# A three-block ConvFFN: operands prepared in steps through DRAM, fewer weight pieces kept, weights loaded one unit ahead

## The chip, the core and the metric

The kernel runs on one core of a Trainium2 chip. Time is device microseconds (us) of one execution, from 3 runs, given as their median and spread. One further execution was profiled; every row below is of that one. Engines are named as the profile does: PE is TensorE's matmuls, PEld its weight loads, DVE is VectorE, ACT ScalarE, POOL GpSimd, SP SyncE, which here issues the DMAs (transfers).

## The reference

One decoder layer over 2048 prompt tokens and 32 sample tokens, model width 1024, FFN width 3072. What the change touches is the last sub-layer and the final norm:

```python
x = x + oc @ p['w_mem_o']                       # cross-attention's projection
n3 = rmsnorm(x, p['g_ffn'])
g, ffn_state = causal_dwconv(n3 @ p['w_ffn_gate'], ffn_prev, p['w_ffn_conv'], p['b_ffn_conv'])
x = x + (jax.nn.gelu(g) * (n3 @ p['w_ffn_up'])) @ p['w_ffn_down']
...
y_prompt = rmsnorm(xp, g_final)
```

All of it is float32.

## The kernel before

**Products.** A float32 operand is held as two parts, hi (rounded for TensorE) and lo (the rest). `split` (L77, L81) makes them: hi by ACT, lo by DVE or POOL, which reads the source and hi. `mm3` (L135) multiplies hi·hi, hi·lo and lo·hi, three matmuls a product.

**Phases.** Phase 0 makes the memory's keys and values, phase 1 is the mixer, phase 2 the output projection and cross-attention over four token blocks s = 0 to 3 of 512 (the samples ride along with others). `memo` (the projection `pmo`) ends a phase-2 block: it adds to the residual x, stores it to DRAM (`x2d`, L1183), and POOL sums its squares (`ssum`, L1196); `rstd3` (L1199) turns them into 1/rms and stores that (`r3d`, L1201).

**The FFN** (`phase3`) runs three token blocks, `SB3`: 696, 692 and 660 + 32 tokens. Each has 24 gate units f and 12 down units d; a down takes two gate units' results. The order of a block is f0, f1, f2, d0, f3, f4, d1, and so on to d9 after f20; then f21, f22, f23; blocks 0 and 1 then make the next block's operands (`"n"` in the plan), run d10 and d11, and normalise and store the block (`final`); block 2 ends in `tail`.

A gate unit (`_P3.gate_up`) computes gate and up projection together by a scheme of seven products instead of eight: both halves of the input's width and both halves of the tokens are combined. Its operands are the seven combinations of `BUDDY` (b11, t2, t1, t3, b21, b22, t4) for four k each; its weights are the pieces a11, s2, s1, s3, a12, s4, a22, of which the s are sums and differences of the weights. Each product is 12 matmuls of 346 to 348 columns into PSUM (`pg`); ACT copies two of them out (`u`, `gb`, L1311 and L1321), DVE adds the others (L1294), then come the convolution (`gc`: ACT L1335, DVE L1337), the gelu, the product `up` and its split `ah`, `al`. A down (`_P3.down`) is 96 matmuls into `pd` from four weight pieces; DVE adds the result to the residual `acc` (L1361).

**Operands.** `p3_norm(s)` loads x by `p3_load`, multiplies by gain and 1/rms (L708), forms the combinations (L693) and splits them (every third lo by POOL) into 56 tiles in SBUF that stay for the whole block. For block 0 it is called ahead of everything in `phase3`, with a priority of 400 (`N3_PRIO`).

**Weights.** `piece_stream` yields pieces of 128 x 2 x 512 (hi, lo), and `piece(ahead=4)` holds up to five at hand, over six buffers `wpc`. In block 0 it loads raw weights, splits them, and stores every piece to DRAM (`kept_g`, seven a gate unit; `kept_d`, four a down; L574); in blocks 1 and 2 it loads each piece from there (`again`), 512 KB a piece.

**What sets the order.** The Tile framework schedules the program's operations onto each engine's queue by priority and dependence; each engine, and SP's DMA queue, then runs its queue in order.

Of the kernel before, what the change touches and what calls it, by code (L numbers as in the profile page):

```python
# [45 lines left out]
class _Kernel:  # L46
# [3 lines left out]
    def run(self):  # L50
        nc, tc, I = self.nc, self.tc, self.I
        with ExitStack() as es:
# [12 lines left out]
            with ExitStack() as e2:  # L65
                self.wspl = e2.enter_context(tc.tile_pool(name="wspl", bufs=3))
                self.psa = e2.enter_context(tc.tile_pool(name="psa", bufs=1, space=bass.MemoryType.PSUM))
                self.psb = e2.enter_context(tc.tile_pool(name="psb", bufs=1, space=bass.MemoryType.PSUM))
                self.phase0()
                self.phase1()  # L70
                self.phase2()
# [393 lines left out]
    def phase2(self):  # L465
        with ExitStack() as es:
# [31 lines left out]
            smp = _MemSample(self)  # L498
            for s in range(4):
# [13 lines left out]
                step(SMO)  # L513
                p.qproj(1)
                step(SMO)
                p.score(0)
# [3 lines left out]
                step(SMO)  # L520
                p.score(1)
                p.trans(0)
                p.qproj(3)
                step(SMO)
                p.score(2)
# [3 lines left out]
                step()  # L529
                p.score(3)  # L530
# [3 lines left out]
                step()  # L534
                p.trans(3)
                p.pv(2)
                nx(2)
                step()
                p.pv(3)
                nx(3)  # L540
                step()
                for u in range(4):
                    p.memo(u)
                    step()
                step()
# [3 lines left out]
                p.rstd3()  # L549

    def piece_stream(self):

# [4 lines left out]
        def load(src):  # L557
            raw = self.wraw.tile([128, 1024], F, name="wr", tag="wr")
            nc.sync.dma_start(raw, src)
            return raw[:, 0:512], raw[:, 512:1024]  # L560
# [6 lines left out]
        def new():  # L567
            return self.wpc.tile([128, 2, 512], R, name="pc", tag="pc")
# [8 lines left out]
        def again(key):  # L577
            t = new()
# [3 lines left out]
        def paired(f):  # L582
            a11, a12 = load(I["w_gate"][f])
            a21, a22 = load(I["w_up"][f])
            yield halves(("g", f, 0), a11, "pool")
            s1 = sums(a21, a22, OP.add)
            s2 = sums(s1, a11, OP.subtract)
            yield halves(("g", f, 1), s2, "dve")
            yield halves(("g", f, 2), s1, "pool")
            yield halves(("g", f, 3), sums(a11, a21, OP.subtract), "dve")  # L590
            yield halves(("g", f, 4), a12, "pool")
            yield halves(("g", f, 5), sums(a12, s2, OP.subtract), "dve")
            yield halves(("g", f, 6), a22, "pool")

        def plain(c):
            raws = [load(I["w_down"][c * CH + i]) for i in range(CH)]
            for h in range(2):
                for i in range(CH):
                    yield halves(("d", c, h * CH + i), raws[i][h], "pool")

        for kind, i in self.units:
            n = 7 if kind == "g" else 2 * CH
            if (kind, i, 0) in kept:
                for e in range(n):
                    yield again((kind, i, e))
            else:
                yield from paired(i) if kind == "g" else plain(i)
# [10 lines left out]
    def phase3(self):  # L618
        nc, tc, I, O = self.nc, self.tc, self.I, self.O
        NC = NF // CH  # L620
        with ExitStack() as es:
# [12 lines left out]
            self.n3 = [None] * 3  # L634
            with tc.high_priority(N3_PRIO):
                self.n3[0] = self.p3_norm(0)
# [4 lines left out]
            for s in range(3):  # L641
# [5 lines left out]
                if s < 2:  # L647
                    plan += [("n", s + 1, 0), ("d", s, NC - 2), ("d", s, NC - 1), ("f", s, 0)]
# [3 lines left out]
            for kind, s, i in plan:  # L652
                if kind == "g":
                    if i == 0:
                        sb = _P3(self, s)
                    acts[i] = sb.gate_up(i)
                    if i == 1:
                        sb.load_acc()
                elif kind == "d":
                    sb.down([acts[i * CH + e] for e in range(CH)])  # L660
                elif kind == "n":
                    self.n3[s] = self.p3_norm(s)
                else:
                    sb.final()
            sb.tail([acts[NF - CH + e] for e in range(CH)])

    def p3_load(self, s, k):
        t0, w, smp = SB3[s]
        W = w + (NS if smp else 0)
        if s and k % 4 > 1:  # L670
            x = self.wraw.tile([128, W], F, name="x3", tag="wr")
        else:
            x = self.xs.tile([128, W], F, name="x3", tag="x", bufs=4)
        self.p3_dma(x, [d[k] for d in self.x2d], t0, W)
        return x
# [9 lines left out]
    def p3_norm(self, s):  # L685
        nc, q1 = self.nc, self.xs
# [3 lines left out]
        rt = q1.tile([128, W], F, name="rt3")  # L690
        self.p3_dma(rt, self.r3d, t0, W)
        self.n3n, ops = 0, {}
# [11 lines left out]
        def norm(k):  # L704
            xs = []
            for kk in (k, k + KT // 2):
                x = self.p3_load(s, kk)
                nc.vector.scalar_tensor_tensor(x, x, self.col(G_FFN, kk), rt, op0=OP.mult, op1=OP.mult)  # L708
                xs += [x[:, 0:H], x[:, H:W]]
            return xs  # L710

        def steps(k, b11, b12, b21, b22):
            put("b11", k, b11)
            t1 = q1.tile([128, H], F, name="t3", tag="t", bufs=4)
            sub(t1, b12, b11)
            sub(b12, b22, b12)
            sub(b11, b12, b11, OP.add)
            yield
# [12 lines left out]

        if s == 0:
            for k in range(KT // 2):
# [809 lines left out]
```

## Time and profile before

| | |
|---|---|
| runs, median (lowest to highest) | 2776.86 us (2772.53 to 2779.53) |
| the profiled execution: time, span | 2779.39 us, 2777.5 us |
| mean granted TensorE clock | 0.969 |
| busy share of the span: PE, DVE, ACT, POOL | 94%, 56%, 34%, 20% |
| moved by DMA | 619.88 MB, mean 223 GB/s |
| chain that ended last, by engine | PE 72%, DVE 13%, DMA 4%, ACT 4%, issue 3% |

The span is the profiled execution from its first to its last instruction; 1.9 us lie around it. Busy shares are averages over all stages. The chain is the work that ended last, followed back from the end, step by step, to whatever released each piece; "issue" is time in which an engine waited for nothing that the profile shows.

### The profile page before, as it was taken

What the parts mean: (1) busy time and instruction counts of PE and PEld (TensorE: products, weight loads), DVE (VectorE), ACT (ScalarE), POOL (GpSimd) and SP (SyncE); (2) the same over time, 40 slices, a digit from 0 to 9 for tenths busy, and PEclk for the clock granted to TensorE, in tenths of its full rate; (3) what the DMA queues carried; (4) which work ended last, traced back from release to release, by engine and by line L of the source; (5) the groups of instructions that cost most, each with busy time, mean ns of one, the idle gap of its engine ahead of it and who ended that gap; (6) DMA issues with size and microseconds to landing.
All of it is one profiled execution on the core that took longest, in us unless ns stands there. A gap on an engine that the chain in (4) does not pass through costs nothing.

```text
span 2777.5 us, 40472 instructions
## 1 busy us (share of the span) xinstructions
PE 2620.8 (94%) x15221; PEld 2414.7 (87%) x15221; DVE 1556.6 (56%) x2735; ACT 945.0 (34%) x1831; POOL 543.7 (20%) x586
## 2 busy tenths in 40 slices
PE   6999998998999996999999978999999989999997
PEld 5777877977998884899999978999999889999997
DVE  6567776676442536767666674544444644444445
ACT  5464735475332434343434342111111321111112
POOL 3422312022402013333333351000000300000001
PEclk9899999999999997999999989999999999999999
DMA  6764544367757565787777758666676576676664
GB/s 244 258 220 147 174 159 151 135 232 252 272 173 247 183 210 181 262 298 273 300 270 292 278 211 284 226 219 220 211 232 209 170 269 223 209 233 211 215 223 147
DMA packets 211650, 619.88 MB, mean 223 GB/s; under 512 B 30404, under 2 KB 51140, under 8 KB 211456
## 3 DMA queue, kind: packets, MB, share of 16 engines
q1 hardware_dynamic: 211456, 617.30, 64.1%
q8 instruction: 121, 1.98, 0.3%
q14 instruction: 73, 0.60, 0.1%
HBM read 442.31 MB, written 174.90 MB: 222 GB/s over the span
## 4 chain that ended last, share of the span: by engine, by line
PE 72%; DVE 13%; DMA 4%; ACT 4%; issue 3%; POOL 2%; SPq 1%; POOLq 0%; ACTq 0%; DVEq 0%
PE pg L135 27%; PE pd L135 17%; PE pin L135 9%; PE po L135 6%; PE pmo L135 3%; PE pq L135 3%; DVE gc L1337 2%; PE sc L135 1%; ACT gc L1335 1%; DVE n L81 1%; POOL pc L81 1%; PE tp L804 1%; DVE pc L81 1%; DVE gb L1294 1%; PE pa L135 1%
## 5 line engine op out<-in xcount | busy, mean ns | idle before, releaser
L135 PE MATMUL pg<-n,pc 128*128 128x346 f32 (+1 forms) x6048 | 1036.7, 330 | 55.4 <-DVE up L1294 18.5
L135 PEld LDWEIGHTS pg<-n,pc 128*128 128x128 f32 x6048 | 979.6, 192 | 101.4 <-DVE up L1294 31.1
L135 PE MATMUL pd<-ah,pc 128*128 128x346 f32 (+1 forms) x2240 | 468.9, 325 | 21.4 <-DVE acc L1361 21.3
L135 PEld LDWEIGHTS pd<-ah,pc 128*128 128x128 f32 x2240 | 378.5, 191 | 29.1 <-DVE acc L1361 27.0
L1361 DVE TENSOR_TENSOR acc<-pd,acc 128x692 f32<-128x692 f32 (+1 forms) x280 | 245.4, 877 | 150.4 <-PE pd L135 149.9
L135 PE MATMUL pd<-al,pc 128*128 128x346 f32 (+1 forms) x1120 | 272.4, 324 | 0.0
L135 PE MATMUL pin<-n1h,wh 128*128 128x512 f32 (+1 forms) x560 | 188.5, 363 | 14.6 <-DVE ql L81 8.7
L135 PEld LDWEIGHTS pd<-al,pc 128*128 128x128 f32 x1120 | 197.0, 191 | 0.0
L81 POOL TENSOR_TENSOR pc<-wr,pc 128x512 fp32r<-128x512 f32 x120 | 161.2, 1346 | 156.5 <-ACT pc L77 147.9
L1337 DVE SCALAR_TENSOR_TENSOR gc<-gb,pp,gc 128x696 f32<-128x696 f32 (+2 forms) x144 | 147.1, 1021 | 79.6 <-ACT gc L1335 77.1
L135 PE MATMUL pin<-n1l,wh 128*128 128x512 f32 (+1 forms) x560 | 186.6, 359 | 4.7 <-DVE n1l L81 4.7
L135 PE MATMUL pin<-n1h,wl 128*128 128x512 f32 (+1 forms) x560 | 185.8, 358 | 2.6 <-POOL wl L81 1.7
L1331 POOL COPY fcarry<-gb 128x2 f32<-128x2 f32 x72 | 14.2, 198 | 875.0 <-DVE gb L1294 873.7
L1294 DVE TENSOR_TENSOR up<-pg,u 128x346 f32<-128x346 f32 (+1 forms) x144 | 74.2, 515 | 148.6 <-PE pg L135 148.6
L1294 DVE TENSOR_TENSOR u<-pg,u 128x346 f32<-128x346 f32 (+1 forms) x144 | 74.5, 518 | 141.6 <-PE pg L135 140.4
L1321 ACT ACTIVATE gb<-pg 128x346 f32<-128x346 f32 (+1 forms) x72 | 33.2, 461 | 338.4 <-PE pg L135 338.4
L135 PEld LDWEIGHTS pin<-n1h,wh 128*128 128x128 f32 x560 | 103.6, 194 | 32.5 <-DVE ql L81 9.3
L1311 ACT ACTIVATE u<-pg 128x346 f32<-128x346 f32 (+1 forms) x72 | 32.5, 452 | 285.4 <-PE pg L135 285.2
L1294 DVE TENSOR_TENSOR gb<-pg,u 128x314 f32<-128x314 f32 (+2 forms) x96 | 38.9, 426 | 160.1 <-PE pg L135 160.1
L81 POOL TENSOR_TENSOR wl<-wr,wh 128x1024 fp32r<-128x1024 f32 x35 | 85.9, 2461 | 208.5 <-ACT wh L77 193.1
L135 PEld LDWEIGHTS pin<-n1l,wh 128*128 128x128 f32 x560 | 103.1, 194 | 19.9 <-DVE n1l L81 5.8
L135 PEld LDWEIGHTS pin<-n1h,wl 128*128 128x128 f32 x560 | 103.1, 194 | 18.7 <-POOL wl L81 2.1
(319 smaller groups left out, 4203.4 us busy)
## 6 DMA issues: line engine op xcount, KB each, us to landing
pc<-kept_g SPq DMA_DIRECT2D x336, 512.0 KB, 4.3
kept_g<-pc SPq DMA_DIRECT2D x168, 512.0 KB, 3.1
pc<-kept_d SPq DMA_DIRECT2D x96, 512.0 KB, 4.4
wh<-keeph SPq DMA_DIRECT2D x90, 512.0 KB, 3.7
wl<-keepl SPq DMA_DIRECT2D x90, 512.0 KB, 4.7
kept_d<-pc SPq DMA_DIRECT2D x48, 512.0 KB, 3.6
x<-in_x_dram SPq DMA_DIRECT2D x72, 256.0 KB, 5.0
keeph<-wh SPq DMA_DIRECT2D x30, 512.0 KB, 3.5
```

Of the source, the lines that this page charges most:

```text
L81: e.tensor_tensor(out=lo, in0=src, in1=hi.bitcast(F), op=OP.subtract)
L135: nc.tensor.matmul(o, w[a], xs, start=first and n == 0, stop=last and n == 2, skip_group_check=more)
L804: nc.tensor.transpose(tp[:, j], st[:, j, c * 128:(c + 1) * 128], K.ident)
L1294: add = lambda o, p, t: nc.vector.tensor_tensor(out=o, in0=p, in1=t, op=OP.add)
L1311: nc.scalar.activation(u, X, AF.Copy)
L1321: nc.scalar.activation(gb[:, 2:2 + H], X, AF.Copy)
L1331: nc.gpsimd.tensor_copy(self.carry[:, f], gb[:, w:w + 2])
L1335: nc.scalar.activation(gc, gb[:, 2:2 + NW], AF.Identity, scale=K.col(C_FW, 48 + f), bias=K.col(C_FB, f))
L1337: nc.vector.scalar_tensor_tensor(gc, gb[:, k:k + NW], K.col(C_FW, 24 * k + f), gc, op0=OP.mult, op1=OP.add)
L1361: nc.vector.tensor_tensor(out=v, in0=pd[:, :, 0:H], in1=v, op=OP.add)
```

## The change

- **Operands ahead, in steps.** `p3_norm` becomes `p3_prep(s)`, a generator of 32 steps that writes the split combinations to DRAM (`opd{s}_{i}`, one per combination) through two-buffer tiles `n3s`. Block 0's steps run inside phase 2, in its blocks s = 2 and 3; those of block s+1 inside the gate units 4 to 19 of FFN block s, after products 1 and 4 of each.
- **Loaded by product.** `p3_ops(s, i)` loads one whole operand (128 x 8 x H, 1.42 MB) in one DMA: for block 0 at the FFN's start, for the others after the product of f23 that last reads the old one.
- **Weights.** Only the four sums of a gate unit are kept in DRAM (`kept_s`). a11, a12, a22 and all down pieces are loaded raw and split at every use, hi by ACT and lo by POOL; later blocks load only the second half of w_up. `raws` loads a unit's raw weights during the unit before.
- **Norms in steps.** The last down of blocks 0 and 1 takes the sums of squares (`sums`); `final` and the 1/rms of phase-2 block 3 (`rstd3_steps`) run as steps after the products of the next gate units 0 and 1.
- **Space.** Phase 2's `yraw` moves to the `wraw` buffers, `ssum3` of its last block to a new pool `prep`, which also holds 1/rms and one combination.

The core of the diff:

```diff
 def phase2(self):
+            self.xpool = lambda: dict(pool=self.wraw, tag="wr")
+            ready = self.p3_prep(0)
+
+            def prep(n=1):
+                if s > 1:
+                    for _ in range(n):
+                        next(ready, None)
                 p.qproj(0)
                 step(SMO)
+                prep()
...
-                p.rstd3()
+                if s < 3:
+                    p.rstd3()

 def piece_stream(self):
-        def halves(key, src, lo_eng):
-            t = new()
+        def halves(src, lo_eng):
+            t = self.wpc.tile([128, 2, 512], R, name="pc", tag="pc")
             self.split(src, t[:, 0], t[:, 1], "act", lo_eng)
+            return t
+
+        def keep(key, src, lo_eng="dve"):
+            t = halves(src, lo_eng)
             kept[key] = self.dram.tile([128, 2, 512], F, name="kept_" + "_".join(map(str, key)))
             nc.sync.dma_start(kept[key], t.bitcast(F))
             return t
...
+            if ("s", f, 0) in kept:
+                yield halves(a11, "pool")
+                for e in range(3):
+                    yield again(("s", f, e))
+                yield halves(a12, "pool")
+                yield again(("s", f, 3))
+                yield halves(u, "pool")
+                return
...
+        nxt = raws(*self.units[0])
+        for n, (kind, i) in enumerate(self.units):
+            now, nxt = nxt, None
+            for t in paired(i, *now) if kind == "g" else plain(now):
+                yield t
+                if nxt is None and n + 1 < len(self.units):
+                    nxt = raws(*self.units[n + 1])

 def phase3(self):
             with tc.high_priority(N3_PRIO):
-                self.n3[0] = self.p3_norm(0)
+                for i in range(7):
+                    self.p3_ops(0, i)
...
-                    plan += [("n", s + 1, 0), ("d", s, NC - 2), ("d", s, NC - 1), ("f", s, 0)]
+                    plan += [("d", s, NC - 2), ("d", s, NC - 1)]
...
                     if i == 0:
+                        rest = sb.final() if s else self.p2[3].rstd3_steps()
+                        ready = self.p3_prep(s + 1) if s < 2 else iter(())
                         sb = _P3(self, s)
-                    acts[i] = sb.gate_up(i)
+
+                    def after(e, s=s, i=i):
+                        if i < 2:
+                            next(rest, None)
+                        elif 4 <= i < 20 and e % 3 == 1:
+                            next(ready, None)
+                        if s < 2 and i == NF - 1:
+                            self.p3_ops(s + 1, e)
+
+                    acts[i] = sb.gate_up(i, after)

+    def p3_ops(self, s, i):
+        H = self.opd[s][0].shape[2]
+        t = (self.n3a if i < 2 else self.n3b).tile([128, KT, H], R, name=f"n3_{i}")
+        self.nc.sync.dma_start(t.bitcast(F), self.opd[s][i])
+        self.n3[i] = t

-    def p3_norm(self, s):
+    def p3_prep(self, s):
         def put(nm, k, src):
-            hl = []
-            for e in "hl":
-                n = BUDDY.index(nm) * 8 + k * 2 + "hl".index(e)
-                hl.append((self.n3a if n < 26 else self.n3b).tile([128, H], R, name=f"n3_{n}"))
-            self.split(src, hl[0], hl[1], "act", "pool" if self.n3n % 3 == 0 else "dve")
-            self.n3n += 1
-            ops[nm, k] = hl
+            nonlocal n
+            t = tile_([128, 2, H], R, "n3s")
+            self.split(src, t[:, 0], t[:, 1], "act", "pool" if n % 3 == 0 else "dve")
+            n += 1
+            nc.sync.dma_start(self.opd[s][BUDDY.index(nm)][:, 2 * k:2 * k + 2], t.bitcast(F))

 class _P3
         def down(self, acts, sums=False):
...
+            if sums:
+                self.tot = K.sumsq(K.xs, acc[:, m], self.tot if m else None, self.W, tags=(("x", 4),) * 2)

     def final(self):
-        tot = None
-        for m in range(KT):
-            tot = K.sumsq(K.xs, acc[:, m], tot, self.W, tags=(("x", 4),) * 2)
-        rt = K.rstd(K.xs, tot, self.W, "pd", "rt3")
+        rc = K.rstd_cols(K.xs, self.tot, self.W, "pd")
+        yield
+        rt = K.rstd_rows(K.xs, rc, self.W, "pd", "rt3")
+        yield
         for m in range(KT):
             nc.vector.scalar_tensor_tensor(acc[:, m], acc[:, m], K.col(G_FIN, m), rt, op0=OP.mult, op1=OP.mult)
             nc.sync.dma_start(K.O["y"][m, :, self.t0:self.t0 + self.W], acc[:, m])
+            yield
```

How the engines' queues change, at three places. First SP at the end of phase 2 and the start of the FFN: `x2d` are stores of the residual, `rt` and `x` loads for the operands. Before:

```order
L1183 DMA x2d_70<-x_6_9845 128x512
L681 DMA rt_10503<-r3d_71 128x512
L681 DMA rt_10503<-r3d_72 128x184
L681 DMA x_10506<-x2d_67 128x512
L681 DMA x_10506<-x2d_68 128x184
L681 DMA x_10510<-x2d_67 128x512
L681 DMA x_10510<-x2d_68 128x184
```

Of the change, `n` being the operand tiles:

```order
L1224 DMA x2d_70<-x_7_9993 128x512
L680 DMA fst<-in_ffn_conv_dram 128x384
L607 DMA kept_s_0_10705<-pc 128x1024
L728 DMA n_2_10668<-opd_2_8859 128x2784
L728 DMA n_3_10670<-opd_3_8860 128x2784
L728 DMA n_4_10672<-opd_4_8861 128x2784
L728 DMA n_5_10674<-opd_5_8862 128x2784
L728 DMA n_6_10676<-opd_6_8863 128x2784
```

The loads of x and 1/rms for the first operands have left this place; operands 2 to 6 are loaded behind the last store of the residual, and operands 0 and 1 stand some twenty rows earlier.

Second DVE at the end of FFN block 0, from gate unit 23 into the last two downs. Before:

```order
L1294 TENSOR_TENSOR up<-pg,u_15735 128x348
L1337 SCALAR_TENSOR_TENSOR gc<-gb,pp,gc 128x696
L1361 TENSOR_TENSOR acc<-pd,acc 128x696
L708 SCALAR_TENSOR_TENSOR x_15862<-x_15862,pp,rt_15843 128x692
L1339 TENSOR_TENSOR up<-up,gc 128x696
L708 SCALAR_TENSOR_TENSOR x_15866<-x_15866,pp,rt_15843 128x692
L708 SCALAR_TENSOR_TENSOR x_15870<-x_15870,pp,rt_15843 128x692
L81 TENSOR_TENSOR al<-up,ah 128x696
L708 SCALAR_TENSOR_TENSOR x_15874<-x_15874,pp,rt_15843 128x692
L81 TENSOR_TENSOR n_5_15895<-x_15862,n_4_15894 128x346
L693 TENSOR_TENSOR t_15898<-x_15862 128x346
```

Of the change:

```order
L1387 SCALAR_TENSOR_TENSOR gc<-gb,pp,gc 128x696 x2
L1342 TENSOR_TENSOR up<-pg,u_15719 128x348
L1411 TENSOR_TENSOR acc<-pd,acc 128x696
L1389 TENSOR_TENSOR up<-up,gc 128x696
L1411 TENSOR_TENSOR acc<-pd,acc 128x696
L83 TENSOR_TENSOR al<-up,ah 128x696
L1411 TENSOR_TENSOR acc<-pd,acc 128x696 x14
```

The norm (L708), the combinations (L693) and the lo halves (L81 on `n`) that stood among and behind the gate unit's last steps are gone from here, and the downs' accumulates follow each other.

Third ACT in FFN block 1, around a gate unit's end, where the steps for block 2 run. Before:

```order
L1338 ACTIVATE gc<-gc 128x692
L77 ACTIVATE ah<-up 128x692
L1311 ACTIVATE u<-pg 128x346
L1321 ACTIVATE gb<-pg 128x346
L1335 ACTIVATE gc<-gb,pp 128x692
```

Of the change:

```order
L1388 ACTIVATE gc<-gc 128x692
L79 ACTIVATE ah<-up 128x692
L79 ACTIVATE n3s<-x_16859 128x346
L79 ACTIVATE pc<-wr 128x512
L79 ACTIVATE n3s<-x_16859 128x346
L79 ACTIVATE n3s<-t_16927 128x346
L1361 ACTIVATE u<-pg 128x346
L79 ACTIVATE pc<-ws 128x512
L79 ACTIVATE pc<-wr 128x512
L79 ACTIVATE n3s<-x_16859 128x346
L79 ACTIVATE n3s<-x_16864 128x346
L1371 ACTIVATE gb<-pg 128x346
```

Hi halves of weight pieces (`pc`) and of operands (`n3s`) now stand among the copies out of PSUM.

## Rows read from the trace of the kernel before

**Rows 1.** The page's list of engines, busy time with its share of the span and the number of instructions.

```profile
PE 2620.8 (94%) x15221; PEld 2414.7 (87%) x15221; DVE 1556.6 (56%) x2735; ACT 945.0 (34%) x1831; POOL 543.7 (20%) x586
```

**Rows 2.** The trace in windows cut at the stages (end of phase 2; FFN start; block 0; its end; start of block 1; block 1; start of block 2). Columns: window, its length, busy time with number of instructions of PE, PEld (TensorE's weight loads), DVE, ACT, POOL, then the granted TensorE clock, the busy share of the DMA engines and GB/s.

```profile
1010.00:1073.00 63.00, 61.82 (x311) 50.48 (x310) 29.53 (x68) 24.69 (x60) 8.56 (x7) 1.00 0.36 131
1073.00:1176.00 103.00, 73.45 (x366) 65.21 (x365) 79.68 (x105) 42.97 (x77) 39.44 (x38) 0.78 0.72 260
1176.00:1580.00 404.00, 394.01 (x2380) 376.64 (x2380) 270.88 (x370) 157.59 (x254) 149.66 (x145) 1.00 0.77 285
1580.00:1676.00 96.00, 78.14 (x443) 75.16 (x442) 65.41 (x90) 41.47 (x74) 49.72 (x39) 0.89 0.60 221
1676.00:1748.00 72.00, 64.72 (x374) 61.37 (x373) 36.85 (x52) 14.26 (x21) 4.64 (x9) 0.95 0.82 286
1748.00:2139.00 391.00, 389.02 (x2377) 380.07 (x2376) 177.78 (x246) 61.12 (x90) 6.63 (x36) 1.00 0.66 218
...
2221.00:2294.00 73.00, 62.90 (x371) 59.92 (x370) 33.60 (x53) 14.08 (x20) 5.24 (x14) 0.95 0.77 258
```

**Rows 3.** The chain of waits over the whole span, its longest pieces: start, duration, what. `pmo` is the last memory projection of phase 2, `pd` a down unit, `pg` a gate unit's product.

```profile
1055.64 17.81 PE pmo L135 x77
...
1171.98 4.31 PE pd L135 x24
...
1575.83 4.09 PE pd L135 x24
...
1648.75 27.64 PE pd L135 x156
...
1733.10 15.25 PE pd L135 x96
...
1777.30 14.56 PE pd L135 x91
...
2124.93 14.56 PE pd L135 x91
...
2191.50 29.59 PE pd L135 x168
...
2280.24 14.30 PE pd L135 x90
...
2714.03 14.30 PE pd L135 x90
```

**Rows 4.** The same chain between the last memory projection and the first operands.

```profile
1075.41 1.71 POOL ssum L1196
...
1087.13 2.02 DMA r3d<-rt
```

**Rows 5.** Groups of instructions by form from 1073 to 1116 us, where the first operands are made: line, engine, operation, out<-in, shapes and count, then busy us, mean ns of one, and the idle time before them with what ended it.

```profile
L77 ACT ACTIVATE n<-x 128x348 fp32r<-128x348 f32 x24 | 10.9, 486 | 21.3 <-DMA r3d<-rt 9.1 <-DVE x L693 9.1 <-DVE x L708 3.0
...
L81 POOL TENSOR_TENSOR n<-x,n 128x348 fp32r<-128x348 f32 x9 | 9.9, 1108 | 20.2 <-ACT n L77 18.6 <-DMA acc<-x2d 1.5
L81 DVE TENSOR_TENSOR n<-x,n 128x348 fp32r<-128x348 f32 x15 | 9.8, 680 | 0.1
L708 DVE SCALAR_TENSOR_TENSOR x<-x,pp,rt 128x696 f32<-128x696 f32 x8 | 8.5, 1059 | 0.0
L693 DVE TENSOR_TENSOR x<-x,x 128x348 f32<-128x348 f32 x8 | 4.8, 603 | 0.1
```

**Rows 6.** Three stretches of 10 us, one at the FFN start and two at the start of block 1; columns as in rows 2.

```profile
1690.00:1700.00 10.00, 8.02 (x37) 7.49 (x38) 5.08 (x7) 0.84 (x2) 0.00 (x0) 0.83 1.00 366
...
1720.00:1730.00 10.00, 7.58 (x45) 6.91 (x44) 1.84 (x4) 0.46 (x1) 0.00 (x0) 1.00 1.04 392
...
1090.00:1100.00 10.00, 4.92 (x12) 3.18 (x12) 9.60 (x14) 5.13 (x13) 5.42 (x5) 0.50 0.66 228
```

**Rows 7.** The chain at the end of block 0.

```profile
1644.04 3.00 DVE n L81 x7
...
1647.90 0.80 DVE acc L1361
```

**Rows 8.** A wait in the steady part of block 0 (1313 to 1580 us): who waited, and for whom, us in total, times, longest.

```profile
PEld pd L135 <- DVE acc L1361: 5.2, 10, 1.2
```

**Rows 9.** Groups by form in the same stretch of block 0, six periods; columns as in rows 5.

```profile
L81 POOL TENSOR_TENSOR pc<-wr,pc 128x512 fp32r<-128x512 f32 x61 | 80.8, 1325 | 92.4 <-ACT pc L77 91.7
...
L1361 DVE TENSOR_TENSOR acc<-pd,acc 128x696 f32<-128x696 f32 x49 | 42.8, 874 | 5.6 <-PE pd L135 5.6
L77 ACT ACTIVATE pc<-wr 128x512 fp32r<-128x512 f32 x60 | 37.7, 629 | 69.5 <-issue 28.5 <-PE pg L135 21.8 <-PE pd L135 11.9
...
L1337 DVE SCALAR_TENSOR_TENSOR gc<-gb,pp,gc 128x696 f32<-128x696 f32 x24 | 27.4, 1143 | 13.6 <-ACT gc L1335 13.2
...
L81 DVE TENSOR_TENSOR al<-up,ah 128x696 fp32r<-128x696 f32 x12 | 12.0, 1001 | 5.2 <-ACT ah L77 5.1
```

**Rows 10.** The same groups of DVE in block 1 (1792 to 2053 us), six periods.

```profile
L1361 DVE TENSOR_TENSOR acc<-pd,acc 128x692 f32<-128x692 f32 x49 | 43.0, 878 | 34.7 <-PE pd L135 34.5
...
L1337 DVE SCALAR_TENSOR_TENSOR gc<-gb,pp,gc 128x692 f32<-128x692 f32 x24 | 22.6, 940 | 14.7 <-ACT gc L1335 14.2
...
L81 DVE TENSOR_TENSOR al<-up,ah 128x692 fp32r<-128x692 f32 x12 | 10.5, 875 | 5.1 <-ACT ah L77 5.1
```

**Rows 11.** The page's list of DMA issues: out<-in, queue, kind and count, KB each, median us from issue to landing.

```profile
kept_g<-pc SPq DMA_DIRECT2D x168, 512.0 KB, 3.1
```

More of the change, by code (lines that the diff above doesn't have):

```diff
@@ L559, in load, with raws @@
             nc.sync.dma_start(raw, src)
-            return raw[:, 0:512], raw[:, 512:1024]
+            return raw
+        def raws(kind, i):
+            if kind == "d":
+                return [load(I["w_down"][i * CH + e]) for e in range(CH)]
+            g = load(I["w_gate"][i])
+            if ("s", i, 0) not in kept:
+                return g, load(I["w_up"][i])
+            u = self.wsum.tile([128, 512], F, name="ws", tag="ws")
+            nc.sync.dma_start(u, I["w_up"][i][:, 512:1024])
+            return g, u
         def sums(x, y, op):
@@ L577, in again, with paired @@
         def again(key):
-            t = new()
+            t = self.wpc.tile([128, 2, 512], R, name="pc", tag="pc")
             nc.sync.dma_start(t.bitcast(F), kept[key])
             return t
[L582 to L585, printed above, removed]
+        def paired(f, g, u):
+            a11, a12 = g[:, 0:512], g[:, 512:1024]
+            if ("s", f, 0) in kept:
[6 more added lines that the diff above has]
+                return
+            a21, a22 = u[:, 0:512], u[:, 512:1024]
+            yield halves(a11, "pool")
@@ L601, in piece_stream @@
[L601 to L607, printed above, removed]
+            yield keep(("s", f, 0), s2)
+            yield keep(("s", f, 1), s1, "pool")
+            yield keep(("s", f, 2), sums(a11, a21, OP.subtract))
+            yield halves(a12, "pool")
+            yield keep(("s", f, 3), sums(a12, s2, OP.subtract))
@@ new lines, in paired, with plain @@
+            yield halves(a22, "pool")
+        def plain(rs):
+            for h in range(2):
+                for r in rs:
+                    yield halves(r[:, h * 512:h * 512 + 512], "pool")
+        nxt = raws(*self.units[0])
[5 more added lines that the diff above has]
+                    nxt = raws(*self.units[n + 1])
@@ L730, in steps @@
             put("t4", k, b21)
-        if s == 0:
-            for k in range(KT // 2):
-                for _ in steps(k, *norm(k)):
-                    pass
-        else:
-            runs = [steps(k, *x) for k, x in enumerate([norm(k) for k in range(KT // 2)])]
-            for _ in BUDDY:
-                for r in runs:
-                    next(r, None)
-        return ops
+            yield
 class _Swa:
@@ L1298, in product @@
             hi, lo = K.piece()
+            x = K.n3[i]
             for k in range(KT // 2):
                 ws = [t[:, k * 128:(k + 1) * 128] for t in (hi, lo)]
-                K.mm3([out], ws, [[t] for t in self.ops[BUDDY[i], k]], first and k == 0, k == KT // 2 - 1, not first)
+                K.mm3([out], ws, [[x[:, 2 * k]], [x[:, 2 * k + 1]]], first and k == 0, k == KT // 2 - 1, not first)
+            after(i)
         gb = q2.tile([128, NW + 2], F, name="gb")
@@ L1347, in gate_up, with down @@
         return ah, al
-    def down(self, acts):
+    def down(self, acts, sums=False):
         K, nc, H, acc = self.K, self.K.nc, self.H, self.acc
```

79 lines of the change are left out of this document (39 added, 40 removed).

## The prediction

> **What bounds the kernel now.** I read the page first: TensorE (PE) is busy for 94% of the span [rows 1], so time can only come from the stretches where it is not. The windows by stage show which these are [rows 2]. In the steady part of FFN block 1 PE works 389.0 of 391 us; in the 103 us at the start of the FFN 73.5, in the 96 us at the end of block 0 78.1, in the 72 and 73 us at the starts of blocks 1 and 2 64.7 and 62.9. Those four are what the change is about.
>
> The chain of waits [rows 3] gives the edges, each as start plus duration: last memory projection 1073.45; d0 of block 0 ends 1176.29, its d9 1579.92, its d11 1676.39; d0 of block 1 1748.35, its d9 2139.49, d11 2221.09; d0 of block 2 2294.54, the last regular down 2728.33. A period is two gate units and one down. Block 1: (2139.49 − 1748.35)/9 = 43.46 us; the down is 14.56 [rows 3], so a gate unit is 14.45. Ideal start of a block (three gate units, one down): 57.9. Ideal end (three gate units, two downs): 72.5. What each stretch costs over that: FFN start 102.8 − 57.9 = **44.9**; end of block 0 96.5 − 72.5 = 24.0 and start of block 1 72.0 − 57.9 = 14.0, together **38.0**; end of block 1 9.1 and start of block 2 15.5, together **24.6**. Block 0's period is 44.85, that is 9 × 1.39 = 12.5 over block 1's. All told 120 us, and no theory of this change can give back more.
>
> [...] At the starts of blocks 1 and 2 it is transfers: 366 and 392 GB/s [rows 6].
>
> **Term by term**, against the profiled execution (2779.4 us; the median of the runs is 2.5 lower).
>
> *FFN start.* Removed: the rstd store, the loads of x behind it, and all DVE, ACT and POOL work for the first operands (the groups of [rows 5]). In the new order operands 0 and 1 are loaded ahead of the last memory projection, but operands 2 to 6 stand on SP behind the stores of that projection, and operand 2 needs the space of what POOL's last addition reads, which ended 3.7 us after the projection [rows 4]. So: five loads of 1.42 MB, 7.1 MB, from about +5 us, at 366 to 392 GB/s [rows 6] 18 to 19 us, the last at +24; with the last products and the low clock after a wait the first gate unit ends at +27 to +33, d0 43.4 later at +70 to +76, instead of +102.8. I take **+27** (the late end, since a low clock follows a wait [rows 6]). Bounds: +32, and +20 if the loads get only the 260 GB/s of that whole stretch [rows 2] (27 us) and PE stays at the low clock.
>
> *Making the operands ahead.* A block has 28 combinations, every third with its lo half on POOL. By [rows 5] that is on DVE 18 lo halves × 680 ns = 12.2 us, 8 norms × 1059 = 8.5, 16 sums × 603 or more = 9.6 up: at least 30.3, I take 33; on ACT 28 × 486 = 13.6; on POOL 10 × 1108 = 11.1. For block 0 they go beside phase 2, where DVE is busy 29.5 of 63 us [rows 2]; PE is not bound by DVE there: **−4** (0 to −10). For blocks 1 and 2 they go beside the steady parts of blocks 0 and 1. What a microsecond of DVE costs there: block 0 has 270.9 − 177.8 = 93 us more of it than block 1 [rows 2] and is 12.5 slower, 0.134 each; part of it is seen as PE's weight loads waiting for accumulates, 5.2 us in 267 [rows 8]. 33 us more: **−4** in block 0 (0 to −12, if the slope steepens as DVE fills), the same in block 1 (below).
>
> *Boundaries.* Removed: the DVE chain of [rows 7], and in the kernel's own order the norm after gate unit 23; sums of squares move into the last down, and the last norm into the next block's first two gate units, one row of y after each product. Added: seven operand loads (9.9 MB), each behind the product that last reads its space. I leave 10.5 us of the 38.0: **+28** (20 to 34); and 10 of the 24.6: **+15** (8 to 21). What is late next is a transfer. From gate unit 23 to the next d0 I count 29.5 MB (operands 9.9, y 2.9, residual 2.8, raw and kept weights 13.9) in an ideal 86.9 us: 340 GB/s, under the 392 that were reached [rows 6], over the 260 to 286 that whole stretches average [rows 2]. Hence ends between nearly nothing left and some 18.
>
> *Weights in blocks 1 and 2.* A gate unit loads 0.52 + 0.26 + 4 × 0.52 = 2.9 MB instead of 3.7, a down 1.0 instead of 2.1. In the steady part transfers bind nothing (218 GB/s, PE at 99%) [rows 2], so the bytes saved buy nothing. Added per period: ten splits, ten times 629 ns on ACT (6.3 us) and 1325 ns on POOL (13.3 us) [rows 9]; both engines have room (61 and 7 of 391 us [rows 2]). But DVE's instructions with two inputs in SBUF were slower where POOL was busy: gc 1143 against 940 ns, al 1001 against 875, while acc, with one input in PSUM, took 874 against 878 [rows 9, 10]. That is 2 × 203 + 126 = 532 ns a gate unit; for some 39 units 21 us of DVE, at 0.134 3 us; with block 1's operands **−7** (0 to −26). [...] The trace shows 126 to 203 ns where one lo half lasts 1325, so mostly no block.
>
> *Stores of the operands.* 56 splits in blocks 0 and 1 put their hi half on ACT, and most wait until the store two puts back has landed; a store of this kind took 3.1 us to land [rows 11]. Behind the waiting ACT instruction stand u<-pg and gb<-pg, which let PE use the PSUM again. Steps come about 7 us apart, so the hold is usually over: 0.15 us each, **−8** (0 to −84). *Tail*: its pieces are split now instead of loaded, **−1**.
>
> Sum: 27 − 4 − 4 + 28 + 15 − 7 − 8 − 1 = 46, so 2733 against the profiled execution and 2731 against the median: **2732**. With each term moved within its nearer bounds 2705 to 2752.
>
> **Rivals.**
> A, the forecast: .55.
> B, POOL and DVE in each other's way: blocks 1 and 2 run at block 0's period. For: gc and al above. Against: block 0 has sums and lo halves on DVE that the later blocks will not have. 19 periods × 1.39 = 26, of which 7 is charged: 2751. .15. [...]
> C, boundaries bound by transfers: 29.5 MB at 285 or 260 GB/s [rows 2] take 104 to 113 us, 17 to 27 over the ideal instead of 10: 6 to 16 more at each, 2744 to 2764. For: both block starts are transfers already. Against: block 1 to 2 has no stores of pieces beside it. .12.
> D, slower: ACT's order is the bound. The new order shows up to five puts between an ah and a gb, closer than the average, and two buffers: each then holds ACT for a landing. At 1.5 us each reaching PE, 56 × 1.5 = 84 instead of 8: 2808; slower than 2785 from (2785 − 2724)/56 = 1.1 us. Against: ACT is 84% idle in block 1 [rows 2], and products in two PSUM tiles give it slack. .11.
> E, nearly all gaps vanish: +32, +31, +19, no toll of DVE or ACT: 2702. .07.
> That the change doesn't do what it says is in part so: at the start five of seven operands come no earlier than the projection's end; it is priced above.
>
> **The numbers.** A measurement of this kernel tells 0.3%, 8.3 us, from no change: "same" is 2768.5 to 2785. A and E are faster (.62); of B and C (.27) about .08 meet each other or small holds (2752 + 12 to 32) and land within it, .19 are faster; D is slower. Faster .81, same .08, slower .11. The range 2697 to 2776 leaves out D and the lower part of E, some .16.
>
> **What would show it.** Right: first gate unit over by 33 us after the last memo; operands 2 to 6 on SP back to back after POOL's addition; no L693/L708 work after gate unit 23; 10 to 20 us between ideal and real at both boundaries, with DMA over 340 GB/s; a period of 43.5 to 43.9 in blocks 1 and 2 with acc near 875 ns. Wrong: a period near 44.8 in block 2 (B); PE waiting for n loads in gate unit 0 of blocks 1 and 2 (C); ACT's n3s waiting on stores and PE waiting behind for u or gb (D). The forecast is most exposed at the boundaries, where 43 of its 46 us arise against a rate that no whole stretch has held.

## The result, and the profile after

| | before | changed |
|---|---|---|
| median (lowest to highest), 4 runs each | 2776.15 us (2772.53 to 2779.53) | 2749.19 us (2743.96 to 2755.25) |
| profiled execution: span, mean granted clock | 2777.5 us, 0.969 | 2748.9 us, 0.977 |

Ratio 0.9895, 95% interval 0.9877 to 0.9913: faster by 27 us, where 2732 was forecast, 44 to 45 faster. The time is in the range and just inside the forecast's own 2705 to 2752; 17 us of the gain are missing.

The page after, and the windows at the changed kernel's own stages, which answer to [rows 1, 2] (columns as there):

```profile
PE 2610.3 (95%) x15221; PEld 2408.1 (88%) x15221; DVE 1583.2 (58%) x2735; ACT 1086.4 (40%) x2071; POOL 863.1 (31%) x826
```

```profile
1077.00:1154.00 77.00, 63.82 (x368) 59.79 (x369) 49.69 (x63) 29.45 (x49) 28.69 (x25) 0.96 0.77 291
1154.00:1573.00 419.00, 398.81 (x2381) 380.77 (x2381) 307.91 (x407) 169.97 (x281) 164.02 (x156) 0.99 0.54 192
1573.00:1646.00 73.00, 71.44 (x437) 69.25 (x436) 42.14 (x56) 29.82 (x47) 33.24 (x30) 1.00 0.77 295
1646.00:1714.00 68.00, 63.72 (x375) 61.48 (x374) 36.75 (x50) 22.73 (x36) 24.74 (x23) 0.95 0.75 255
1714.00:2121.00 407.00, 392.23 (x2378) 382.39 (x2377) 206.87 (x275) 125.99 (x208) 131.62 (x135) 0.99 0.55 180
2121.00:2194.00 73.00, 72.32 (x446) 70.72 (x445) 33.12 (x43) 25.10 (x40) 31.34 (x30) 1.00 0.76 284
2194.00:2267.00 73.00, 64.72 (x379) 62.09 (x378) 37.06 (x54) 22.03 (x35) 25.81 (x29) 0.95 0.65 211
2267.00:2700.00 433.00, 428.37 (x2641) 419.86 (x2640) 195.65 (x301) 128.29 (x200) 152.92 (x179) 1.00 0.48 156
```

Read the lengths first. The start went from 103 to 77 us and the end of block 0 from 96 to 73, but the "steady" parts of blocks 0 and 1 grew from 404 to 419 and from 391 to 407, PE idle for 20 and 15 us in them (10 and 2 before [rows 2]).

All kernels side by side, us, cut at the end of the last matmul of each down (the start begins at the last memory projection's end):

| kernel | start | block 0 | its end | start 1 | block 1 | its end | start 2 | block 2 | ratio to before (95%) |
|---|---|---|---|---|---|---|---|---|---|
| before | 102.9 | 403.6 | 96.5 | 72.0 | 391.1 | 81.6 | 73.5 | 433.8 | 1 |
| changed | 77.1 | 419.1 | 73.7 | 67.8 | 407.0 | 73.0 | 72.2 | 433.2 | 0.9895 (0.9877–0.9913) |
| e1_no_making | 76.2 | 399.9 | 73.7 | 67.5 | 390.4 | 73.0 | 73.8 | 432.7 | 0.9771 (0.9752–0.9790) |
| e2_no_store | 75.8 | 417.2 | 73.8 | 67.9 | 399.6 | 73.0 | 73.5 | 433.0 | 0.9866 (0.9848–0.9884) |
| e3_paced | 75.7 | 415.0 | 73.7 | 67.4 | 394.5 | 72.9 | 74.0 | 432.6 | 0.9834 (0.9818–0.9850) |
| e8_paced_lo_pool | 77.9 | 429.2 | 77.2 | 66.3 | 394.7 | 73.0 | 73.5 | 432.8 | 0.9926 (0.9911–0.9940) |
| e11_paced_wsum4 | 78.3 | 426.4 | 73.9 | 68.0 | 394.5 | 73.0 | 73.7 | 432.8 | 0.9907 (0.9890–0.9924) |
| e10_in_downs | 74.9 | 401.6 | 73.7 | 67.6 | 391.8 | 73.0 | 73.8 | 432.7 | **0.9796** (0.9783–0.9810) |
| e12_raw_at_use | 88.7 | 400.6 | 79.0 | 66.9 | 391.7 | 73.0 | 73.6 | 432.7 | 0.9850 (0.9819–0.9881) |
| e5_all_kept | 81.2 | 437.2 | 74.4 | 73.3 | 392.1 | 83.6 | 74.1 | 432.2 | 0.9998 (0.9988–1.0008) |
| e7_kept_no_making | 81.6 | 410.7 | 73.8 | 76.0 | 389.6 | 86.3 | 70.7 | 432.1 | 0.9896 (0.9880–0.9911) |
| e6_made_at_start | 97.2 | 408.4 | 73.7 | 66.4 | 406.6 | 73.0 | 73.2 | 433.2 | 0.9939 (0.9923–0.9956) |
| e9_norm_at_once | 76.2 | 418.3 | 73.7 | 72.0 | 402.9 | 73.2 | 76.1 | 432.8 | 0.9905 (0.9883–0.9926) |

Each row is one profiled execution. Where kernels are alike the steady blocks agree within some 1 us (block 1 of e3_paced and e8_paced_lo_pool 394.5 and 394.7), the starts within 3.4 (74.9 to 78.3).

Where the loss sits is plainer by period. In the changed kernel block 0's nine take 52.8, 48.1, 51.0, 46.4 and then 44.1 to 44.3; block 1's 50.3, 49.1, 47.3 and then 43.4. The operand splits `n3s` run in just those: this view gives, for block 0 and then block 1, count, shortest, median and longest ns, first and last start:

```profile
L79 ACT ACTIVATE n3s<-x x24: 477/486/498, 1158.3 to 1315.1; 128x346 fp32r<-128x346 f32 x24
...
L79 ACT ACTIVATE n3s<-x x23: 476/494/499, 1716.5 to 1827.2; 128x346 fp32r<-128x346 f32 x23
```

The source puts two steps into each of gate units 4 to 19. The built order had them in units 3 to 9: an engine's queue is filled with whatever is ready, and the steps were ready early.

### The profile page after: what moved, and what is told of

The parts are those of the page before. It is cut to its first block, busy times and chain, and to the rows that moved or that the text cites. A ratio compares the mean times of both kernels' runs of the same rounds, so it can differ in the third digit from the quotient of the medians.

```text
span 2748.9 us, 40952 instructions
## 1 busy us (share of the span) xinstructions
PE 2610.3 (95%) x15221; PEld 2408.1 (88%) x15221; DVE 1583.2 (58%) x2735; ACT 1086.4 (40%) x2071; POOL 863.1 (31%) x826
## 4 chain that ended last, share of the span: by engine, by line
PE 70%; DVE 11%; DMA 5%; ACT 4%; issue 4%; POOL 3%; SPq 1%; POOLq 0%; DVEq 0%; ACTq 0%
PE pg L137 24%; PE pd L137 17%; PE pin L137 9%; PE po L137 6%; PE pq L137 3%; PE pmo L137 3%; DVE gc L1387 3%; PE sc L137 1%; POOL pc L83 1%; DMA opd<-n3s 1%; ACT gc L1385 1%; PE tp L845 1%; DVE ws L596 1%; DMA x<-x2d 1%; PE msc L137 1%
## 5 line engine op out<-in xcount | busy, mean ns | idle before, releaser
L83 POOL TENSOR_TENSOR pc<-wr,pc 128x512 fp32r<-128x512 f32 x312 | 415.6, 1337 | 497.3 <-ACT pc L79 491.3
L79 ACT ACTIVATE pc<-wr 128x512 fp32r<-128x512 f32 x312 | 195.5, 629 | 504.2 <-PE pd L137 240.8
L83 POOL TENSOR_TENSOR pc<-ws,pc 128x512 fp32r<-128x512 f32 x72 | 94.3, 1309 | 183.3 <-ACT pc L79 163.6
L79 ACT ACTIVATE pc<-ws 128x512 fp32r<-128x512 f32 x144 | 89.9, 627 | 117.6 <-PE pg L137 68.1
```

What stands on the lines that cost most here:

```text
L79: nc.scalar.activation(hi, src, AF.Copy)
L83: e.tensor_tensor(out=lo, in0=src, in1=hi.bitcast(F), op=OP.subtract)
```

## The experiments

**Is the making the cause?** The operands of blocks 1 and 2 are not made.

```diff
-                        ready = self.p3_prep(s + 1) if s < 2 else iter(())
+                        ready = iter(())
...
-        self.nc.sync.dma_start(t.bitcast(F), self.opd[s][i])
+        self.nc.sync.dma_start(t.bitcast(F), self.opd[0][i][:, :, 0:H])
```

> Leaves out the making of the operands of FFN blocks 1 and 2 (they load block 0's stored operands instead, so y of those blocks is of the wrong tokens). The four or five slow periods at the start of blocks 0 and 1 (52.8, 48.1, 51.0, 46.4 and 50.3, 49.1, 47.3 us against 44.1 and 43.4 later) cost 21.7 + 16.4 = 38 us. Theory H (the making holds the queues of ACT and DVE): all 38 go, about 2711 (2704 to 2718), with 44.1 and 43.4 us from the second down on. Rival W (only DVE's work counts, 33 us a block at the forecast's 0.134): 9 go, about 2740. Rival R (the raw weights loaded a unit ahead and the stores of sums make the slow periods): under 5 go, 2744 to 2750.

Block 0 got 19.2 us shorter and block 1 16.6, and but for block 0's first (46.2) every period is 44.0 to 44.4 and 43.4: **the making costs 35.8 us**, its toll below, all of the slow periods. W and R fall.

**Is it the stores' landing?** As e1, but the steps run, without their stores.

```diff
-            nc.sync.dma_start(self.opd[s][BUDDY.index(nm)][:, 2 * k:2 * k + 2], t.bitcast(F))
+            if s == 0:
+                nc.sync.dma_start(self.opd[s][BUDDY.index(nm)][:, 2 * k:2 * k + 2], t.bitcast(F))
```

> The operands of blocks 1 and 2 are made, but not stored (blocks 1 and 2 load block 0's). Theory H: an n3s buffer is free when its lo half is done instead of when its store has landed, so ACT and the instructions behind it are not held; the loads of x stay: some 20 to 30 of the 38 us go, 2719 to 2729. Rival W (DVE's work, made in a bunch): nothing goes, 2744 to 2752. Rival X (the loads of x hold DVE): under 10 go, 2740 to 2748.

Only 1.9 and 7.4 us came back. The steps ran denser (block 0: two periods of 55.2 and 53.4, then 43.8 to 44.3). So a landing holds ACT (2.9 us in the third row below), but it is not what costs most; theory H, as stated, fell. By the time alone rival X (the loads of x hold DVE) would be met, but DVE waited for no load of x in block 0's slow stretch and 4.2 us in block 1's. What PE waits for in the slow stretch of block 0 (1154 to 1340 us; us in total, times, longest) says so too:

```profile
PE pg L137 <- DVE gb L1342: 8.3, 8, 2.8
...
PE pg L137 <- DVE u L1342: 5.5, 7, 2.1
...
ACT n3s L79 <- DMA opd<-n3s: 2.9, 3, 2.1
...
PE pg L137 <- DVE up L1342: 2.5, 5, 1.1
```

PE waits for DVE's additions that empty PSUM, hardly for ACT (0.9 us). In block 1's slow stretch ACT does wait for stores, 15.0 us, but PE still for DVE's `gb` (5.8) and `up` (4.4).

**Does spreading them help?** Each step's instructions are ordered behind the last addition (DVE) or copy (ACT) of the gate unit, without a semaphore.

```diff
+    def pin(self, b):
+        a = self.anchor.get(b.ins.engine)
+        if a is not None:
+            self.tc.add_manual_dep(b.ins, a.name, mybir.DependencyInfo(mybir.DependencyClass.NoSync, mybir.DependencyReason.DATA), reason="pace")
+        return b
...
-        add = lambda o, p, t: nc.vector.tensor_tensor(out=o, in0=p, in1=t, op=OP.add)
+        add = lambda o, p, t: mark(nc.vector.tensor_tensor(out=o, in0=p, in1=t, op=OP.add))
```

> Everything is made and stored, but each step's instructions on DVE and ACT are ordered behind the last copy or addition that its gate unit gave that engine before the step, so that the steps run two to a gate unit over sixteen units, where the built order put them into seven. Theory H with bunching: a store has about 14 us to land before its buffer is wanted, and the toll falls from 38 to 4 to 12 us: 2715 to 2724. Rival W (work is work, wherever it stands): 2744 to 2752. Theory H without bunching (every landing reaches PE, 56 times some 0.7 us): 2740 to 2752.

The steps are spread now (`n3s` in block 0 from 1177 to 1536 us). The result lies between the theories: block 1's toll fell from 16.6 to 4.1 us, block 0's only from 19.2 to 15.1. Windows of blocks 0 and 1, paced and then without the making:

```profile
1157.00:1571.00 414.00, 393.48 (x2376) 376.89 (x2375) 309.86 (x406) 169.79 (x280) 168.59 (x155) 1.00 0.54 194
1713.00:2107.00 394.00, 387.76 (x2375) 377.67 (x2374) 205.65 (x276) 125.10 (x208) 137.00 (x136) 1.00 0.57 187
```

```profile
1159.00:1558.00 399.00, 392.69 (x2377) 376.84 (x2376) 270.74 (x364) 158.83 (x252) 148.30 (x145) 1.00 0.47 171
1700.00:2090.00 390.00, 386.92 (x2375) 377.74 (x2374) 175.53 (x234) 115.08 (x180) 121.39 (x127) 1.00 0.49 158
```

In block 1 the making adds 30.1 us of DVE for 4.1 us of time, 0.136 each: the forecast's price. In block 0 it adds 39.1 for 15.1, 0.39 each.

**Is block 0's DVE too full, or held?** Two edits that made it slower. First, in the paced kernel, the lo halves of the sums go to POOL:

```diff
-        def keep(key, src, lo_eng="dve"):
+        def keep(key, src, lo_eng="pool"):
```

> The paced kernel, and block 0's lo halves of the sums (three a gate unit, 0.77 us each on DVE) go to POOL. Block 0's making still cost 15 us when paced (415 against 399.9 us without), in block 1 4 us. If that is DVE's share (310 of 414 us busy): DVE loses 42 us of work and block 0 comes down to 399 to 406 us, 9 to 16 us in all, ratio to the kernel before 0.978 to 0.980. If it is POOL that slows DVE's two-input instructions (al 999 to 1252 ns there already): POOL has 73 us more, DVE's instructions stretch and nothing is won, block 0 412 us or more, ratio 0.983 or more.

Worse, 429 us, though DVE's own work fell from 310 to 293: its sums waited 27.2 us for POOL to free a buffer, where 11.4 was the paced kernel's, with the additions behind them, and `ws<-wr,ws` took 1329 ns where the paced kernel's took 777.

```profile
DVE ws L597 <- POOL pc L84: 27.2, 27, 1.6
```

Second, a fourth buffer for the sums:

```diff
-            self.wsum = pool("wsum", 3)
+            self.wsum = pool("wsum", 4)
```

> The paced kernel with four buffers for the sums of weights instead of three. With lo halves moved to POOL, sums on DVE waited for POOL's lo halves to free a buffer (27 us in 433), 11.4 us in 414 in the paced kernel. If it is this wait, in DVE's own order, that puts the additions late in block 0: 415 goes to 403 to 409 us, ratio 0.979 to 0.982. If DVE is only full: 413 to 416, ratio 0.983 to 0.985.

Worse as well, 426 us: with the buffer the built order changed, and PE waited 14.3 us for `gb` alone (8.8 paced). The sums' wait for POOL is gone there, without a gain; but as the order changed with it, the run doesn't tell what that wait had cost, and why this order is worse than the paced one was not settled.

**Is it the place?** Four steps to a down, behind every second addition of downs 1 to 8.

```diff
-                        elif 4 <= i < 20 and e % 3 == 1:
-                            next(ready, None)
...
+            b = nc.vector.tensor_tensor(out=v, in0=pd[:, :, 0:H], in1=v, op=OP.add)
+            K.anchor[b.ins.engine] = b.ins
+            if m % 2:
+                next(ready, None)
```

> The paced kernel with its steps in another place: four to a down, behind every second addition of downs 1 to 8, instead of two to a gate unit. Without the making DVE is busy 12.4 of 14.4 us in a gate unit of block 0 (86%: 3.5 for sums, 2.3 for lo halves, 6.6 for the rest), 7.0 of 14.6 in a down (48%). If the 15 us that the paced making still costs in block 0 come from DVE having no room inside gate units: 415 goes to 400 to 406 us, block 1's 394.5 stays or loses up to 3, ratio to the kernel before 0.977 to 0.980. If DVE's work costs the same anywhere: 412 to 418, ratio 0.982 to 0.985. If the additions that empty PSUM in a down have less slack than those of a gate unit: slower than paced, 0.985 or more.

Block 0 401.6, block 1 391.8: **of 35.8 us of toll 3.1 are left**, with the same instructions. PE's waits in its block 0 (1152 to 1554 us):

```profile
PE pg L138 <- DVE up L1351: 3.3, 9, 0.4
...
PE pd L138 <- DVE acc L1420: 2.2, 4, 0.8
...
PE pg L138 <- DVE u L1351: 1.3, 1, 1.3
```

And in the paced kernel's (1157 to 1571 us):

```profile
PE pg L138 <- DVE gb L1353: 8.8, 10, 1.3
PE pg L138 <- DVE u L1353: 7.7, 7, 1.6
PE pg L138 <- DVE up L1353: 3.3, 9, 0.4
PE pd L138 <- DVE acc L1422: 0.2, 1, 0.2
```

So the place decides. But the reason is not the one expected, that gate units have no room and downs have. The expectation's 12.4 of 14.4 us books each instruction to the unit that it belongs to, and weight pieces are made up to five ahead, many of them while PE is at a down. Cut by time, DVE is busier in the downs. These are sums over block 0 without the making (e1_no_making), first of its 18 gate units, then of its nine downs, each down from its seventh matmul to its last (length, then busy time):

```profile
sum 260.50, PE 254.80 PEld 241.57 DVE 161.90 ACT 122.16 POOL 135.07; mean PE 28.31 PEld 26.84 DVE 17.99 ACT 13.57 POOL 15.01
```

```profile
sum 139.40, PE 138.79 PEld 136.17 DVE 109.34 ACT 36.94 POOL 13.85; mean PE 15.42 PEld 15.13 DVE 12.15 ACT 4.10 POOL 1.54
```

DVE is busy 62% of the first and 78% of the second, POOL 52% and 10%. At most 63 of DVE's 109 us in the downs can be accumulates (72 in the block, at a mean of 878 ns). With the steps in them, in e10_in_downs, DVE is busy 126 of the downs' 143 us. Two things go with the low price in the downs. The making adds less busy time to DVE, 27.4 and 23.9 us in blocks 0 and 1 where it added 39.1 and 30.1 paced; POOL, beside whose additions some of DVE's instructions took longer (last section), is nearly idle there. And PE hardly waits for the additions that the steps stand beside. No run takes the two apart. This version beats both kernels: 2720.08 us against 2776.71 for the one before in the same set of runs.

**The weights' part.** All pieces kept and loaded again:

```diff
-            if ("s", f, 0) in kept:
-                yield halves(a11, "pool")
...
+            if ("g", f, 0) in kept:
+                for e in range(7):
+                    yield again(("g", f, e))
+                return
```

> Undoes the weights' part alone: all seven pieces of a gate unit and four of a down are stored in block 0 and loaded in blocks 1 and 2, as before the change. If splitting at each use costs nothing where POOL and ACT have room: block 2's period stays at 43.3 to 43.4 us, block 0's late periods go from 44.1 back to some 44.8 (6 us), the block starts, with 29.5 MB grown to 33, lose 0 to 10 each: 2752 to 2772. If POOL's lo halves slow DVE and with it PE (rival B of the prediction): blocks 1 and 2 gain, period under 43.2, 2735 to 2745.

> All weight pieces kept in DRAM as before the change, and the making for blocks 1 and 2 left out (they load block 0's operands, so y of those blocks is of the wrong tokens). With all pieces kept, block 0's steady part took 437 us with the making, 403.6 in the kernel before, which had none of it. If the making and the stores of the pieces are in each other's way (DVE, and SP's queue): 402 to 408 here, so 30 or more of making's toll in place of the 19 it has with sums alone kept. If raw weights a unit ahead are what slows it: 425 or more. The ends and starts of blocks stay as with all kept (83.6 and 73.3 us), if it is the pieces' bytes that lengthen them; the time 2735 to 2745 on a chip where the kernel before takes 2780.

(The second is the first with e1's edit.) Both forecasts of the time were missed: 2780.92 us, and 2749.95 with block 0 at 410.7, between the two values given. Block 2's period stays, 43.2 against 43.3, so splitting at each use costs next to nothing there (433.2 against 432.2 for the block). Keeping all costs 29 us with the making (0.9998 against 0.9895) and 35 without it (0.9896 against 0.9771): in block 0, where 26.5 us of toll take the place of 19.2, and at the starts and at block 1's end. Block 1 itself got 14.9 us shorter. Beside loaded pieces the making takes 2.5 us there (392.1 against 389.6), beside raw ones 16.6, though its steps are bunched here too, in three and a half periods instead of two and a half (the window of block 1, then ACT's splits as above):

```profile
1749.00:2141.00 392.00, 387.31 (x2377) 377.95 (x2376) 192.38 (x274) 73.22 (x117) 14.56 (x45) 1.00 0.75 248
```

```profile
L79 ACT ACTIVATE n3s<-x x23: 477/495/497, 1751.4 to 1899.3; 128x346 fp32r<-128x346 f32 x23
```

Raw pieces alone cost the block 0.8 us (390.4 against 389.6). So in block 1 neither the bunch nor the splitting costs much by itself; together they do. ACT and POOL are busy 73 and 15 of 392 us in this block with all kept, 126 and 132 of 407 in the changed kernel; which of them matters was not run apart. And in block 0 with all kept the built order spread the steps by itself (`n3s` from 1204 to 1544 us), and they still cost 26.5.

At block 1's end the chain waits for a piece:

```profile
2178.56 15.12 DMA pc<-kept_d
```

This is the chain of e5_all_kept at the end of its block 1. The piece was issued among the operand loads of 1.4 MB.

Loading a unit ahead, by itself, undone on top of e10:

```diff
-        nxt = raws(*self.units[0])
+        for kind, i in self.units:
+            now = raws(kind, i)
+            yield from paired(i, *now) if kind == "g" else plain(now)
```

> The kernel with the steps in the downs, but a unit's raw weights are loaded when its first piece is made (five pieces ahead of use), not during the unit before. With all pieces kept, also loaded five pieces ahead, PE waited at the end of block 1 for pieces of the last downs that stood on SP's queue behind the operand loads: 83.6 us instead of 73.0. If loading ahead is what removed that wait: the ends of blocks 0 and 1 grow from 73.7 and 73.0 to 77 to 84, steady periods stay at 44.3 and 43.3, 6 to 20 us in all, ratio to the kernel before 0.982 to 0.987. If the fewer bytes did it: 0 to 3 us, 0.979 to 0.981. If the raw loads also come late inside the blocks: periods over 45, ratio above 0.99.

It is worth 13.8 us at the start, which no forecast had, and 5.3 at block 0's end, nothing at block 1's end. What is left to explain that one are the raw weights in place of kept pieces, half the bytes of a down; no run takes these apart.

**The start, and the norm.** `prep()` leaves phase 2 and all steps run behind it; in the other, `final` stands behind the last down in one piece, without `sums`.

```diff
-                if s > 1:
+                if s > 3:
...
+            for _ in ready:
+                pass
```

> Undoes one part: block 0's 32 steps all stand behind phase 2 instead of inside it. If making them ahead is what the FFN start gained (25.8 us by the chain: 102.9 to 77.1), the start grows again to 95 to 115 us, while the last memory projection ends 2 to 4 us earlier: 17 to 35 us over the changed kernel, about as long as the kernel before (ratio 0.996 to 1.004). Rival: the start is bound by the transfers of 7 operands and of the first weights anyway, then under 8 us are lost (ratio 0.989 to 0.993).

```diff
-                    plan += [("d", s, NC - 2), ("d", s, NC - 1)]
+                    plan += [("d", s, NC - 2), ("d", s, NC - 1), ("f", s, 0)]
```

> Undoes one part: sums of squares, the last norm and the stores of y of blocks 0 and 1 stand together behind the last down again, the rest as changed. If the steps were part of what the two boundaries gained (26.8 and 9.9 us), starts of blocks 1 and 2 grow from 67.8 and 72.2 us to 72 and 76: 6 to 12 us over the changed kernel (ratio 0.991 to 0.994). If all of it came from the operands: 0 to 3 us (0.989 to 0.9905).

The first start took 97.2 us: making ahead is worth 20 of the 25.8 us won there; the time rose by only 0.44%, some 12 us, as block 0 got 10.7 shorter; why is open. The norm's steps are worth 4.2 and 3.9 us at the starts, as expected; but block 1 got 4.1 shorter without them, and the total, 0.9905 against 0.9895, can't be told from the changed kernel's.

## Why the prediction was right, and where it was not

In all: the start and the boundaries gained 62.5 us of 70 forecast. The making in blocks 0 and 1 cost 35.8 where 16 was forecast, 4 for DVE in each and 8 for the stores. Block 0 gained 3.7 us apart from it (403.6 to 399.9 in e1_no_making).

- **FFN start**, +27 forecast: 25.8. As worked out, five loads were issued behind POOL's addition (SP's timeline: start, duration, what; then the chain, which answers to [rows 4]), and gate unit 0 ended 28.6 us after the projection, where 27 to 33 was given; d0 came 48.5 us behind it, where 43.4 was given.

```profile
1084.06 2.67 SPq L728 DMA_DIRECT2D n<-opd  x5
```

```profile
1082.78 1.26 POOL ssum L1237
...
1084.90 12.87 DMA n<-opd
...
1097.82 2.19 PE pg L137 x12
```

- **Phase 2**, −4: not resolved. The projection ended 3.2 us later than before, but kernels equal up to there ended it anywhere from 1076.6 to 1083.9, and e6_made_at_start, without the steps there, at 1083.9.
- **Boundaries**, +28 and +15: 26.8 and 9.9. What is left over the ideal is 11.1 and 14.8 us. The sign given, DMA over 340 GB/s, did not come: 291 and 261 from gate unit 23 to the next d0. The cause was only half told: the gain was booked to operands and norm, yet with all pieces kept the excess is 17.3 and 27.3 us (147.7 and 157.7 − 130.4), rival C's 17 to 27. "The bytes saved buy nothing" holds in the steady parts of blocks 1 and 2 and fails at the edges.
- **DVE's price for the making**, −4 in block 0 and about as much in block 1, is **the step that failed**. The two blocks lost 15.5 and 15.9 us in all, the making 19.2 and 16.6. The price of 0.134 us a microsecond of DVE came from two whole blocks and was put on work wherever it stands. It came out for block 1 once the steps were spread over gate units (0.136). So spread it was 0.39 in block 0; in the downs it was 0.06 in both. Bunched in block 1 it was 0.53 (16.6 us for 31.3) beside raw pieces and 0.12 (2.5 for 21.6) beside loaded ones. "Steps come about 7 us apart" was read from the source; the third order excerpt showed otherwise.
- **Stores**, −8: 9.3 went with them (e2). The size was right, in part by luck, as its reason, steps 7 us apart, did not hold, and in e2 the steps also ran denser. Rival D's 84 was far off.
- **Splitting at each use**, the rest of the −7: nothing to be seen by itself, block 2 433.2 against 433.8; but the making costs block 1 14.1 us more beside it (16.6 against 2.5). `al` did take longer, in block 2 with raw pieces and with all kept:

```profile
L83 DVE TENSOR_TENSOR al<-up,ah 128x692 fp32r<-128x692 f32 x16 | 16.2, 1013 | 7.2 <-ACT ah L79 6.8
```

```profile
L83 DVE TENSOR_TENSOR al<-up,ah 128x692 fp32r<-128x692 f32 x16 | 14.1, 880 | 6.8 <-ACT ah L79 6.8
```

But DVE is 45% busy there, and PE's matmuls waited 4.5 of 433 us for it. Rival B falls, at its price of 26 us. These means hide two kinds: with raw pieces 8 of the 16 took 879 to 881 ns, none beside an addition of POOL's, and 8 took 1140 to 1152, each begun while a lo half ran on POOL. "Mostly no block" was read off means and was wrong: in the stretch of [rows 9] 6 of 12 `al` (1125 to 1131 ns, the others 866 to 886) and 10 of 24 `gc` (1133 to 1856, the others 942 to 947) had begun beside one.
- **Tail**, −1: 49.2 before, 49.1 after.

## What to carry to other kernels

The price of background work in an engine's queue was set here by where it stood and by what ran beside it: the making in two blocks cost 36 us bunched, 19 spread over gate units and 3 inside downs. The engine's free share did not tell that price, for DVE was busier in the downs than in the gate units (78% against 62%); look for the foreground instructions that get late, how long their waiters can bear it, and what the other engines run beside them. Costs did not simply add: in block 1 bunched making and raw weights cost 2.5 and 0.8 us alone and 17.4 together. Emission order is no pacing: steps written into gate units 4 to 19 were scheduled into 3 to 9, so read the built queue, and tie background steps to the foreground's instructions. Keeping all pieces, and so loading more bytes, cost nothing in block 2 (432.2 against 433.2 us) but 6.2 and 12.5 us more at the two boundaries; in the second the chain waited 15.1 us for a piece issued among loads of 1.4 MB.

## What the runs showed of the hardware

DVE's `al`, with two inputs in SBUF, took longer where it began while POOL ran an addition, and then ended a nearly fixed time behind that addition. From 1150 to 2700 us of the changed kernel 21 of those of 692 columns began so: they took 1033 to 1222 ns and ended 733 to 738 ns behind it, and the 24 beside none took 869 to 881. So too the sum `ws<-wr,ws` in block 0 of e8_paced_lo_pool (count; shortest, median and longest ns; first and last start), and one case from the timeline, behind two lo halves on POOL in a row:

```profile
L597 DVE TENSOR_TENSOR ws<-wr,ws x19: 691/1752/1769, 1163.7 to 1583.7; 128x512 f32<-128x512 f32 x19
```

```profile
1204.38 2.55 POOL L84 TENSOR_TENSOR pc<-ws,pc 128x512 fp32r<-128x512 f32 x2 [4.35 <-ACT pc L80]
...
1205.72 1.76 DVE L597 TENSOR_TENSOR ws<-wr,ws 128x512 f32<-128x512 f32 x1 [0.26 <-POOL pc L84]
```

Of the 19, 7 took 691 to 693 ns and 12 took 1404 to 1769, and each of the 12 had begun while POOL ran a lo half of some 1300 ns. Its mean of 702 ns in e1_no_making, 777 in e3_paced and 1329 in e8_paced_lo_pool counts how often that happened: 1, 3 and 12 of 19. It is not a matter of POOL's load alone: `ws<-wr` went from 996 to 918 and 910 ns in the same three. `acc`, with one input in PSUM, took 878, 879 and 877, beside POOL's additions too: from 1150 to 2700 us of the changed kernel 58 that began beside one took 869 to 885 ns, 209 beside none 865 to 884. Lo halves worth an estimated 42 us (three a gate unit, 0.77 us each), moved from DVE to POOL, took only 17 us off DVE (310 to 293).
